# Two-layer attention trunk on one core: a chunk's last two key blocks are transposed and evicted together

## The chip, the cores and the metric

One core of one Trainium2 chip runs the whole program. The metric is the device time of one execution in microseconds (us). The engines are named as in the profile: PE is TensorE, DVE is VectorE, ACT is ScalarE, POOL is GpSimd, SP is the engine that issues the DMAs; SPq and the like are an engine's queue. PEld is the loading of weights into PE.

## What is computed

The input is 1024 positions of 1024 channels; 16 learned positions are put in front, which makes 1040. Two layers follow. Each one normalizes, projects, runs two kinds of attention heads side by side, gates them with SiLU, projects back and adds to the residual. Cut to what matters here:

```python
# differential heads (4 per layer): two softmaxes, one subtracted from the other
s = einsum(q, k) * scale;  s = where(chunk(k) <= chunk(q), s, -inf)
p = softmax(s);            a = p[:, :, 0] - lam * p[:, :, 1]
do = rmsnorm(a @ v, subln_gain) * (1 - lam_init) * silu(dg)
# forgetting heads (8 per layer): causal, with a cumulative bias
s = einsum(q, k) * scale + c[q] - c[k];  s = where(k <= q, s, -inf)
fo = (softmax(s) @ v) * silu(fg)
h = h + concat(do, fo) @ w_out
```

All of it is float32; the kernel splits most operands of a product into a high and a low part (float32r) and adds two or three products.

## The kernel before, in words

**Tiling.** The 1040 positions are nine blocks, 80 and then seven of 128 and a last one of 64 (`BS`, `BE`, lines 29 and 30). Three blocks are a chunk (`CS`, `CE`): 336, 384 and 320 positions. Eight head pairs are worked through in each layer, pairs 0 to 3 differential and 4 to 7 forgetting. A `Unit` (line 664) is one chunk of queries of one differential head pair, or of one head of a forgetting pair: 12 and 24 units a layer, 72 in all.

**A unit.** `scores` (628) makes the scores of one query block against all its keys on PE, DVE adds the mask or bias, takes the running minimum and evicts (652, 656), and ACT takes the exponential with its row sum (660). For a forgetting head DVE takes the reciprocal (692) and POOL scales the rows (693). For a differential head there are two such passes, m = 0 and m = 1; after the second DVE takes a reciprocal (709), makes one factor per row from it, lambda and the first row sum (710), and combines the two (712). Then, for each key block j of the unit (three, six or nine of them), `transp` (727) turns the probabilities of the unit's query blocks on PE into a PSUM tile `tp`, ACT copies this to `ath`, the high part (743), and DVE subtracts to get `atl`, the low part (744). `av` (748) multiplies both with the values and adds into `po`. A chunk's last two key blocks see only part of the queries. Their products are still 256 columns wide, so POOL fills the missing columns with zeros in `ath` and `atl` (741, 742): once in a unit of the first and the second chunk, and twice in one of the third. `finish` (765) evicts `po` into `ta` tiles, of which there are three (`OB`), applies the gate if it is there already (785), and stores to DRAM (786). `head_sums` (793) makes the differential heads' sums of squares on PE and copies three columns out, one by one (803).

**Gates.** `gate` (581) projects a pair's gate. Where the attention of that chunk is already stored, it loads it into a `ta` tile (`load_o`, 591), multiplies on POOL (619) and stores (620). Otherwise it keeps the gate in a `gs` tile; at most `GB`, 4, are kept (602).

**What sets the order.** PE's instructions are in the order in which the program issues them. `attention` (805) walks through the units: the first two transposes, then products and transposes in turn (line 838 and after), with score steps of the next unit put between them; all the steps are offered by `layer` (1080) one at a time. Between them `layer` puts pieces of the other projections (`fills`, 1023, in the order of `ORDER`), as a planner's clock (`Clock`, 160) and costs (lines 52 to 60) say: it fills until the next step's input is due (`need`). The planner charges 0.088 us at each change between transposes and other matmuls (`TURN`) and says that an eviction is ready 0.7 us after its transposes (`LT`). The other engines work in the order in which their own queues were filled.

Of the kernel before, what the change touches and what calls it, by code (L numbers as in the profile page):

```python
# [8 lines left out]
F32 = mybir.dt.float32  # L9
# [24 lines left out]
CE = [336, 720, T]  # L34
CW = 384

WB, XB, QB, EB, AB, GB, OB, TCB = 8, 4, 8, 6, 2, 4, 3, 3
MW = 512
TB, SB = 2, 3

# [44 lines left out]
def trunk_kernel(ctx, tc, x, meta, norm_gain, w_in, fbias, lq1, lk1, lq2, lk2,  # L85
# [18 lines left out]
    for t, r, a in ((dm, 64, MW - 64), (dm0, N_META, N_META)):  # L104
# [12 lines left out]

    qls = [[cp.tile([P, CE[c] - CS[c]], F32R, name=f"ql{c}{s}") for s in range(2)]
           for c in range(3)]
    dma(out=ident, in_=cst[:, C_ID:C_ID + P])  # L120
    for c in range(3):
        for s in range(2):
            nc.gpsimd.memset(qls[c][s][64 - 64 * s:128 - 64 * s, :].bitcast(F32), 0.0)
# [51 lines left out]
    when = {}  # L175

    def mm(o, a, b, start, stop, passes=1):
        n = b.shape[-1]
        nc.tensor.matmul(o, a, b, start=start, stop=stop)  # L179
        pe.add(b.dtype == BF16, max(n * passes * COL, 0.056))  # L180

# [399 lines left out]
    def gate(l, p, acts, box):  # L581


        g0 = (DG if p < 4 else FG) + (p % 4) * P
        ws = load_w_all(w_in[l], [(g0, g0 + P)])
        parts = 1 if p < 4 else 2

        def finished(p, c):
            return sum((p, c, s) in box["fin"] for s in range(parts))

        def load_o(p, c):
            n = finished(p, c)
            if not n:
                return ()
            w = CE[c] - CS[c]
            o = st("ta", CW, F32, OB)
            dma(out=o[0:n * P // parts, :w], in_=oscr[l, c, p, 0:n * P // parts, 0:w])
            return (o,) * n

        for c in range(3):  # L600
            w = CE[c] - CS[c]
            while box["kept"] >= GB:
                yield True
            there = load_o(p, c)
            mb, c0 = [], skip(l, c)
            yield from mtile(ws, acts, c, mb, c0)
            now = finished(p, c)
            if now > len(there):
                there = load_o(p, c)
            pt = mb[0]  # L610
            th = st("tc", CW)
            nc.scalar.activation(th[:, c0:w], pt[:, c0:w], AF.Tanh, scale=0.5)
            keep = len(there) < parts
            g = st("gs", CW, bufs=GB) if keep else th
            nc.vector.scalar_tensor_tensor(g[:, c0:w], th[:, c0:w], 1.0, pt[:, c0:w],
                                           ALU.add, ALU.mult)
            if there:
                o = there[0][0:len(there) * P // parts, c0:w]
                nc.gpsimd.tensor_tensor(o, o, g[0:o.shape[0], c0:w], ALU.mult)
                dma(out=oscr[l, c, p, 0:o.shape[0], c0:w], in_=o)  # L620
                box["done"]["g", c] = pe.t + 2.0
            if keep:
                box["kept"] += 1
                box["gs", p, c] = g
            yield
# [38 lines left out]
    class Unit:  # L664
# [17 lines left out]
        def score(self, j, m):  # L682
            l, ext = self.l, BE[j]
            if j == self.tiles[-1] and (m if self.diff else self.s):
                self.box["sc_ok"].add((self.p, self.c))
            kt = self.box["k", self.p, self.c]
            q = self.box["q", self.p, self.c]
            if not self.diff:
                cb = self.box["cb", self.s]
                e, l, rows = scores(kt, q, self.s, j, ext, lambda a, b: cb[:, a:b], True)  # L690
                r = st("rl", 2, bufs=6)
                nc.vector.reciprocal(r[rows, 0:1], l[rows, :])  # L692
                nc.gpsimd.tensor_scalar(e[rows, :ext], e[rows, :ext], r[rows, 0:1], 1.0,  # L693
                                        ALU.mult, ALU.mult)
                self.at[j] = e, rows
                self.ready = max(self.ready, pe.t + LS[0][0] + LS[0][1] * ext)
                return

            l0 = self.box["l0"][:, self.p, j:j + 1]

            def bias(a, b):
                return dm0[:, a:b] if j == 0 else dm[:, MW - ext + a:MW - ext + b]
            e, ls, rows = scores(kt, q, m, j, ext, bias, False, l0 if m == 0 else None)
            if m == 0:
                self.e0 = e
                return
            e0 = self.e0
            r = st("rl", 2, bufs=6)
            nc.vector.reciprocal(r[rows, 0:1], ls[rows, :])
            nc.vector.scalar_tensor_tensor(r[rows, 1:2], r[rows, 0:1], neglam[rows, l:l + 1],  # L710
                                           l0[rows, :], ALU.mult, ALU.mult)
            nc.vector.scalar_tensor_tensor(e0[rows, :ext], e[rows, :ext], r[rows, 1:2],
                                           e0[rows, :ext], ALU.mult, ALU.add)
            self.at[j] = e0, rows
            self.ready = max(self.ready, pe.t + LS[1][0] + LS[1][1] * ext)

        def geom(self, j):
            c, w = self.c, self.w
            i0 = max(j, 3 * c)
            n0 = BS[i0] - CS[c]  # L720
            n1 = max(min(n0, w - 256), 0) if j > 3 * c else 0
            return BE[j] - BS[j] + self.pad(j), i0, n0, n1

        def pad(self, j):
            return 64 if j == NB - 1 else 0

        def transp(self, j):
            c, w = self.c, self.w
            kz, i0, n0, n1 = self.geom(j)
            tp = att_ps()  # L730
            for i in self.tiles:
                if i < i0:
                    continue
                e, rows = self.at[i]
                o = BS[i] - CS[c] - self.pad(i)
                tr(tp[:kz, o:BE[i] - CS[c]], e[rows, BS[j] - self.pad(j):BE[j]],
                   ident[rows, rows])
            ah = st("ath", CW, F32R, AB)
            al = st("atl", CW, F32R, AB)
            if n1 < n0:  # L740
                nc.gpsimd.memset(ah[:kz, n1:n0].bitcast(F32), 0.0)
                nc.gpsimd.memset(al[:kz, n1:n0].bitcast(F32), 0.0)
            nc.scalar.activation(ah[:kz, n0:w], tp[:kz, n0:w], AF.Copy)  # L743
            nc.vector.tensor_tensor(al[:kz, n0:w], tp[:kz, n0:w], ah[:kz, n0:w].bitcast(F32),  # L744
                                    ALU.subtract)
            self.ev[j] = (ah, al, pe.t + LT)

        def av(self, j):
            w = self.w
            kz, i0, n0, n1 = self.geom(j)  # L750
            if j == 0:
                self.po = ps.tile([P, 512], F32, name="po", tag="po", bufs=1)
            ah, al, _ = self.ev.pop(j)
            v = self.box["v", self.p, j]
            if self.diff:
                vh, vl = v[:kz, j, 0:P], v[:kz, j, P:2 * P]
# [1 line left out]
            else:  # L758
                vs = v[:kz, j, self.s * P:(self.s + 1) * P]
                prods = ((vs, ah), (vs, al))  # L760
            for n, (a, b) in enumerate(prods):
                mm(self.po[:, n1:w], a, b[:kz, n1:w], j == 0 and n == 0,
                   j == self.nblk - 1 and n == len(prods) - 1)

        def finish(self):

# [24 lines left out]
            return late  # L791

    def head_sums(sq, c, p, box):
        ms = box["ms"][:, p, :]
        box["sums"] += 1
        pt = proj_ps("sc")
        for b in range(3):
            j = 3 * c + b
            n = BE[j] - BS[j] + (64 if j == NB - 1 else 0)
            mm(pt[:n, b:b + 1], sq[:, BE[j] - CS[c] - n:BE[j] - CS[c]], ones, True, True, 4)  # L800
        for b in range(3):
            n = BE[3 * c + b] - BS[3 * c + b] + (64 if 3 * c + b == NB - 1 else 0)
            nc.vector.tensor_copy(ms[:n, 3 * c + b:3 * c + b + 1], pt[:n, b:b + 1])

    def attention(l, box):

# [22 lines left out]
        for i, u in enumerate(units):  # L829
# [4 lines left out]
                free = 2 * free - 1  # L834
            if nx and nx.p != u.p and not nx.diff:
                free = 0
            n = u.nblk
            seq = [("t", j) for j in range(TB)]
            for j in range(n):
                seq.append(("a", j))  # L840
                if j + TB < n:
                    seq.append(("t", j + TB))
            nt = 0
            yield u.ready, ("v", u.p, 0)
            box["vp"] = u.p
            for k, (what, j) in enumerate(seq):
# [4 lines left out]
                    u.transp(j)  # L851
                    nt += 1
                else:
                    yield u.ev[j][2], ("v", u.p, j)
                    u.av(j)
                yield 0.0, None
                if todo and (nt == n or (free > 0 and nt >= FR0 and k % FR1 == FR1 - 1)):
# [19 lines left out]
    def head_norms(l, box):  # L877
# [9 lines left out]
        def turn():  # L887
            pt = proj_ps("sc")
            tr(pt[:36, 0:P], rs, ident)
            rt = st("msr", P, bufs=1)  # L890
            nc.scalar.activation(rt[:36, :], pt[:36, 0:P], AF.Copy)
            for h in range(4):
                for j0, j1 in ((0, 1), (1, 8), (8, 9)):
# [219 lines left out]

    with tc.manual_schedule(engines={mybir.EngineType.PE}):
        acts = [None] * 3
        box = {"done": {}, "sc_ok": set(), "fin": set(), "kept": 0, "sums": 0}
        v0 = v_unit(0, 0, acts, box)
        xs = [first_load(0)]
        next(v0)
# [16 lines left out]
        for l in range(depth):  # L1136
# [2 lines left out]
            layer(l, acts, box, new)  # L1139
            tail = box["tail"]  # L1140
            if l < depth - 1:
                acts, box = new, {"done": {}, "sc_ok": set(), "fin": set(), "kept": 0, "sums": 0}
                v0 = weave(v_unit(l + 1, 0, acts, box), tail)
            else:
                drive(tail)
# [54 lines left out]
```

## Time and profile before

| | us |
|---|---|
| runs of the kernel, median of 3 | 1608.13 (1601.7 to 1608.35) |
| the profiled execution: its time | 1607.66 |
| the profiled execution: its span, first to last instruction | 1605.6 |
| busy DVE, ACT, POOL | 1043.0, 828.6, 689.6 |

The span is what the trace covers; some 2 us lie around it. A busy time is the sum of an engine's instructions. Matmuls are pipelined, so that PE's busy time counts overlaps, and its cost is better read from the starts of neighbours. The granted clock of PE has a mean of 0.973 over the span. The stages are: 0 to 90 us the input and the first values, 90 to 400 differential heads and 400 to 700 forgetting heads of the first layer, to 870 its output projection; then the same again, 870 to 1190, 1190 to 1480 and to the end.

### The profile page before, as it was taken

What the parts mean: (1) busy time and instruction counts of PE and PEld (TensorE: products, weight loads), DVE (VectorE), ACT (ScalarE), POOL (GpSimd) and SP (SyncE); (2) the same over time, 40 slices, a digit from 0 to 9 for tenths busy, and PEclk for the clock granted to TensorE, in tenths of its full rate; (3) what the DMA queues carried; (4) which work ended last, traced back from release to release, by engine and by line L of the source; (5) the groups of instructions that cost most, each with busy time, mean ns of one, the idle gap of its engine ahead of it and who ended that gap; (6) DMA issues with size and microseconds to landing.
All of it is one profiled execution on the core that took longest, in us unless ns stands there. A gap on an engine that the chain in (4) does not pass through costs nothing. (4 is left out here: it accounts for less than half of the span.)

```text
span 1605.6 us, 30162 instructions
## 1 busy us (share of the span) xinstructions
PE 1487.7 (93%) x9932; PEld 1420.1 (88%) x9932; DVE 1043.0 (65%) x3024; ACT 828.6 (52%) x2067; POOL 689.6 (43%) x1125
## 2 busy tenths in 40 slices
PE   5988999999999999988998999899999999888997
PEld 4888989999999999887988899799999999886897
DVE  6488747866755575757655976586756555547564
ACT  6455545545654565543334654465556556446443
POOL 3353233404442445456846341442253344344674
PEclk9999999999999999998999999999999999999999
DMA  9252212223321324555434231332242222335454
GB/s 242 64 113 73 71 51 75 72 36 86 69 66 42 79 67 126 170 151 159 147 70 106 69 87 33 88 81 50 43 93 59 52 69 61 87 96 159 138 158 139
DMA packets 181725, 148.28 MB, mean 92 GB/s; under 512 B 19624, under 2 KB 177120, under 8 KB 181568
## 3 DMA queue, kind: packets, MB, share of 16 engines
q1 hardware_dynamic: 181568, 146.34, 34.6%
q8 instruction: 79, 1.29, 0.3%
q14 instruction: 78, 0.64, 0.1%
HBM read 117.70 MB, written 28.59 MB: 91 GB/s over the span
## 5 line engine op out<-in xcount | busy, mean ns | idle before, releaser
L179 PE MATMUL pj<-acth,whi 128*128 128x320 f32 (+2 forms) x1536 | 517.0, 337 | 22.9 <-ACT tc L416 7.6
L179 PE MATMUL pj<-acth,wlo 128*128 128x320 f32 (+2 forms) x1536 | 498.1, 324 | 2.7 <-POOL wlo L263 2.7
L179 PE MATMUL pj<-actl,whi 128*128 128x320 f32 (+2 forms) x1536 | 497.8, 324 | 0.0
L263 POOL TENSOR_TENSOR wlo<-wst,whi 128x256 fp32r<-128x256 f32 (+1 forms) x320 | 249.3, 788 | 244.0 <-ACT whi L259 216.3
L179 PEld LDWEIGHTS pj<-acth,whi 128*128 128x128 f32 x1536 | 295.9, 193 | 28.0 <-ACT tc L416 8.2
L179 PEld LDWEIGHTS pj<-acth,wlo 128*128 128x128 f32 x1536 | 295.2, 192 | 3.8 <-POOL wlo L263 3.2
L179 PEld LDWEIGHTS pj<-actl,whi 128*128 128x128 f32 x1536 | 293.9, 191 | 0.0
L660 ACT ACTIVATE e<-e,mn 80x80 f32<-80x80 f32 (+8 forms) x288 | 225.2, 782 | 124.2 <-DVE mn L652 121.6
L744 DVE TENSOR_TENSOR atl<-tp,ath 128x320 fp32r<-128x320 f32 (+8 forms) x432 | 191.5, 450 | 97.7 <-ACT ath L743 92.9
L743 ACT ACTIVATE ath<-tp 128x320 fp32r<-128x320 f32 (+8 forms) x432 | 167.6, 403 | 138.2 <-PE tp L183 131.1
L179 PE MATMUL sc<-kt,qq 128*128 128x296 f32 (+9 forms) x480 | 178.8, 375 | 25.2 <-DVE mn L652 17.3
L259 ACT ACTIVATE whi<-wst 128x256 fp32r<-128x256 f32 (+1 forms) x304 | 124.1, 415 | 150.4 <-DMA wst<-in_w_out_dram 50.7
L693 POOL TENSOR_SCALAR e<-e,rl 80x80 f32<-80x80 f32 (+2 forms) x144 | 110.8, 770 | 165.6 <-DVE rl L692 160.2
L183 PE MATMUL tp<-ident,e 128*128 128x128 f32 (+2 forms) x1080 | 180.7, 275 | 0.9 <-POOL e L693 0.8
L179 PE MATMUL po<-ath,v 128*128 128x256 f32 (+5 forms) x576 | 167.1, 331 | 13.2 <-ACT ath L743 9.9
L179 PE MATMUL pj<-whi,acth 128*128 128x256 f32 (+3 forms) x576 | 166.4, 289 | 6.7 <-DVE v L428 5.8
L179 PE MATMUL pj<-wlo,acth 128*128 128x256 f32 (+3 forms) x576 | 164.2, 285 | 2.1 <-POOL wlo L263 1.4
L179 PE MATMUL pj<-whi,actl 128*128 128x256 f32 (+3 forms) x576 | 163.8, 284 | 0.6 <-POOL actl L404 0.6
L179 PE MATMUL sc<-kt,ql 128*128 128x296 f32 (+9 forms) x480 | 159.7, 335 | 0.0
L179 PE MATMUL po<-atl,v 128*128 128x256 f32 (+5 forms) x432 | 136.8, 317 | 12.8 <-DVE atl L744 11.7
L183 PEld LDWEIGHTS tp<-ident,e 128*128 128x128 f32 (+2 forms) x1080 | 137.1, 140 | 7.0 <-POOL e L693 2.3
L179 PEld LDWEIGHTS sc<-kt,qq 128*128 128x128 f32 (+1 forms) x480 | 91.5, 191 | 37.7 <-DVE mn L652 23.8
(166 smaller groups left out, 2471.5 us busy)
## 6 DMA issues: line engine op xcount, KB each, us to landing
wst<-in_w_in_dram SPq DMA_DIRECT2D x256, 128.0 KB
wst<-in_w_out_dram SPq DMA_DIRECT2D x192, 128.0 KB
cb<-cscr SPq DMA_DIRECT2D x16, 520.0 KB
cb<-in_rope_dram SPq DMA_DIRECT2D x20, 320.0 KB
cb<-in_rope_dram SPq DMA_DIRECT2D x16, 384.0 KB
oscr<-ta SPq DMA_DIRECT2D x22, 192.0 KB
oscr<-ta SPq DMA_DIRECT2D x26, 160.0 KB
cb<-in_rope_dram SPq DMA_DIRECT2D x12, 336.0 KB
```

Source lines behind the costliest of these rows:

```text
L179: nc.tensor.matmul(o, a, b, start=start, stop=stop)
L183: nc.tensor.transpose(o, a, idn)
L259: nc.scalar.activation(hi, sg_, AF.Copy)
L263: eng.tensor_tensor(lo, sg_, hi.bitcast(F32), ALU.subtract)
L660: nc.scalar.activation(e[rows, :ext], e[rows, :ext], AF.Exp, scale=-1.0, bias=mn[rows, len(pcs) - 1:len(pcs)], accum_out=l[rows, :])
L693: nc.gpsimd.tensor_scalar(e[rows, :ext], e[rows, :ext], r[rows, 0:1], 1.0, ALU.mult, ALU.mult)
L743: nc.scalar.activation(ah[:kz, n0:w], tp[:kz, n0:w], AF.Copy)
L744: nc.vector.tensor_tensor(al[:kz, n0:w], tp[:kz, n0:w], ah[:kz, n0:w].bitcast(F32), ALU.subtract)
```

## The change

Key blocks n-2 and n-1 of a unit become one group: their transposes go into one PSUM tile side by side (block n-1 behind column w), one ACT copy and one DVE subtraction evict both. The two parts lie in fixed tiles `ats`, in which stretches of zeros are written once at the start; a product that needs zero columns reads them from there, for block n-1 as two stretches of 128 columns. POOL's clearing for each unit goes. The product of lambda and the first row sum is made on POOL after pass m = 0, so that DVE has a reciprocal and a product of two columns left. `head_sums` makes all three columns 128 rows high and copies them with one instruction. A gate loads the stored attention once, after its matmuls and not before them, and `GB` goes from 4 to 3 (2 for the last two chunks of pair 7). `turn` takes its tile from the ring `tc`.

```diff
-WB, XB, QB, EB, AB, GB, OB, TCB = 8, 4, 8, 6, 2, 4, 3, 3
+WB, XB, QB, EB, AB, GB, OB, TCB = 8, 4, 8, 6, 2, 3, 3, 3
...
+    ats = [cp.tile([P, 2 * CW + 192], F32R, name=f"at{i}") for i in range(AB)]
+    AH, AL = 128, CW + 192
     dma(out=ident, in_=cst[:, C_ID:C_ID + P])
+    for t in ats:
+        nc.gpsimd.memset(t[:, 0:AH].bitcast(F32), 0.0)
+        nc.gpsimd.memset(t[:, AL - 64:AL].bitcast(F32), 0.0)
...
-            while box["kept"] >= GB:
+            while box["kept"] >= (GB - 1 if p == 7 and c else GB):
                 yield True
-            there = load_o(p, c)
             mb, c0 = [], skip(l, c)
             yield from mtile(ws, acts, c, mb, c0)
-            now = finished(p, c)
-            if now > len(there):
-                there = load_o(p, c)
+            there = load_o(p, c)
...
             if m == 0:
-                self.e0 = e
+                r = st("rl", 2, bufs=6)
+                nc.gpsimd.tensor_scalar(r[rows, 0:1], l0[rows, :], neglam[rows, l:l + 1], 1.0,
+                                        ALU.mult, ALU.mult)
+                self.e0 = e, r
                 return
-            e0 = self.e0
-            r = st("rl", 2, bufs=6)
-            nc.vector.reciprocal(r[rows, 0:1], ls[rows, :])
-            nc.vector.scalar_tensor_tensor(r[rows, 1:2], r[rows, 0:1], neglam[rows, l:l + 1],
-                                           l0[rows, :], ALU.mult, ALU.mult)
+            e0, r = self.e0
+            nc.vector.reciprocal(r[rows, 1:2], ls[rows, :])
+            nc.vector.tensor_tensor(r[rows, 1:2], r[rows, 1:2], r[rows, 0:1], ALU.mult)
...
-        def transp(self, j):
+        def groups(self):
+            n = self.nblk
+            return [(j,) for j in range(n - 2)] + [(n - 2, n - 1)]
+
+        def transp(self, g):
             c, w = self.c, self.w
             tp = att_ps()
+            n0 = BS[max(g[0], 3 * c)] - CS[c]
+            kz = BE[g[0]] - BS[g[0]]
             for i in self.tiles:
                 e, rows = self.at[i]
                 o = BS[i] - CS[c] - self.pad(i)
+                for j in g:
+                    if i >= j:
+                        oo = o if j == g[0] else w
+                        k0 = BS[j] - self.pad(j)
+                        tr(tp[:kz, oo:oo + BE[i] - CS[c] - o], e[rows, k0:k0 + kz],
+                           ident[rows, rows])
-            ah = st("ath", CW, F32R, AB)
-            al = st("atl", CW, F32R, AB)
-            if n1 < n0:
-                nc.gpsimd.memset(ah[:kz, n1:n0].bitcast(F32), 0.0)
-                nc.gpsimd.memset(al[:kz, n1:n0].bitcast(F32), 0.0)
+            n1 = w if len(g) == 1 else w + BE[g[1]] - BS[g[1]] + self.pad(g[1])
+            t = ats[self.box["at"] % AB]
+            self.box["at"] += 1
+            ah, al = (t[:kz, x:x + n1 - n0] for x in (AH, AL))
+            nc.scalar.activation(ah, tp[:kz, n0:n1], AF.Copy)
+            nc.vector.tensor_tensor(al, tp[:kz, n0:n1], ah.bitcast(F32), ALU.subtract)
...
+                self.ev[g[0]] = (n0 - z, *(t[:kz, x - z:x + w - n0] for x in (AH, AL)), ready)
+            if len(g) == 2:
+                two = []
+                for x in (AH, AL):
+                    v = t[:kz, 0:P]
+                    two.append(bass.AP(v.tensor, v.offset,
+                                       [list(v.ap[0]), [x + w - n0, 2], [1, P]]))
+                self.ev[g[1]] = (w - 256, *two, ready)
...
-        for b in range(3):
-            n = BE[3 * c + b] - BS[3 * c + b] + (64 if 3 * c + b == NB - 1 else 0)
-            nc.vector.tensor_copy(ms[:n, 3 * c + b:3 * c + b + 1], pt[:n, b:b + 1])
+            a = BE[j] - P - CS[c] if j == NB - 1 else BS[j] - CS[c]
+            mm(pt[:, b:b + 1], sq[:, a:a + P], ones, True, True, 4)
+        nc.vector.tensor_copy(box["ms"][:, p, 3 * c:3 * c + 3], pt[:, 0:3])
...
-            n = u.nblk
-            seq = [("t", j) for j in range(TB)]
-            for j in range(n):
-                seq.append(("a", j))
-                if j + TB < n:
-                    seq.append(("t", j + TB))
+            gs = u.groups()
+            n = len(gs)
+            seq = [("t", g) for g in gs[:TB]]
+            for i, g in enumerate(gs):
+                seq += [("a", j) for j in g]
+                if i + TB < n:
+                    seq.append(("t", gs[i + TB]))
```

## Rows read from the trace of the kernel before

**Rows 1.** Busy time of each engine and its share of the span, from the page
```profile
PE 1487.7 (93%) x9932; PEld 1420.1 (88%) x9932; DVE 1043.0 (65%) x3024; ACT 828.6 (52%) x2067; POOL 689.6 (43%) x1125
```

**Rows 2.** Windows view, first differential stage: us, then busy us (instructions) by engine
```profile
90.00:400.00 310.00, 290.16 (x1964) 279.53 (x1962) 228.26 (x683) 162.86 (x414) 105.51 (x161) 0.98 0.28 69
```

**Rows 3.** Waits of PE in attention: total us, times, longest
```profile
PE sc L179 <- DVE mn L652: 17.3, 15, 3.8
PE po L179 <- DVE atl L744: 11.7, 14, 2.3
PE po L179 <- ACT ath L743: 9.9, 7, 3.6
PE sc L179 <- DVE e L656: 6.3, 7, 1.3
PE po L179 <- DVE ta L782: 3.1, 2, 2.4
```

**Rows 4.** Groups by form, PE: products of 256 columns (busy, mean ns, idle before)
```profile
L179 PE MATMUL po<-ath,v 128*128 128x256 f32 x192 | 49.3, 298 | 1.0 <-ACT ath L743 1.0
L179 PE MATMUL po<-atl,v 128*128 128x256 f32 x144 | 40.9, 285 | 1.9 <-POOL atl L742 1.0 <-DVE atl L744 0.8
```

**Rows 5.** Timeline of PE around one lone transpose: start, duration, instruction
```profile
410.47 0.27 PE L183 MATMUL tp<-ident,e 128*128 128x128 f32 x1
410.50 0.38 PE L179 MATMUL sc<-kt,qq 128*128 128x296 f32 x1
410.72 0.30 PE L179 MATMUL sc<-kt,ql 128*128 128x296 f32 x1
410.86 0.30 PE L179 MATMUL sc<-kt,qq 128*128 128x296 f32 x1
```

**Rows 6.** Groups by form, ACT and VectorE: evictions of the transposed blocks
```profile
L743 ACT ACTIVATE ath<-tp 128x384 fp32r<-128x384 f32 x72 | 35.0, 486 | 18.7 <-PE tp L183 17.4 <-DVE mn L652 0.7
L743 ACT ACTIVATE ath<-tp 128x256 fp32r<-128x256 f32 x48 | 18.1, 377 | 3.4 <-PE tp L183 3.1
L743 ACT ACTIVATE ath<-tp 128x128 fp32r<-128x128 f32 x48 | 13.0, 272 | 19.1 <-PE tp L183 18.6
L744 DVE TENSOR_TENSOR atl<-tp,ath 128x384 fp32r<-128x384 f32 x72 | 39.7, 551 | 0.4 <-ACT ath L743 0.2
L744 DVE TENSOR_TENSOR atl<-tp,ath 128x256 fp32r<-128x256 f32 x48 | 20.0, 416 | 1.7 <-ACT ath L743 1.5
L744 DVE TENSOR_TENSOR atl<-tp,ath 128x128 fp32r<-128x128 f32 x48 | 13.7, 285 | 3.5 <-ACT ath L743 3.3
```

**Rows 7.** Groups by form, VectorE: steps of one column
```profile
L710 DVE SCALAR_TENSOR_TENSOR rl<-rl,neglam,l 128x1 f32<-128x1 f32 x64 | 19.1, 299 | 1.3
L803 DVE COPY ms<-sc 128x1 f32<-128x1 f32 x64 | 6.4, 148 | 8.1 <-PE sc L179 8.0
```

**Rows 8.** GpSimd: clearing, its waits, the weights' low part, the gate's product
```profile
L741 POOL MEMSET ath<- 128x128 f32 x48 | 9.9, 206 | 97.2 <-PE po L179 91.8 <-DVE kt L428 3.0 <-DVE mn L652 2.0
POOL ath L741 <- PE po L179: 141.1, 48, 23.6
L263 POOL TENSOR_TENSOR wlo<-wst,whi 128x256 fp32r<-128x256 f32 (+1 forms) x320 | 249.3, 788 | 244.0 <-ACT whi L259 216.3 <-issue 16.1 <-PE pj L179 2.9
L619 POOL TENSOR_TENSOR ta<-ta,tc 128x320 f32<-128x320 f32 x18 | 17.0, 946 | 26.2 <-DMA ta<-oscr 8.0 <-DVE ffz L530 7.5 <-issue 6.1
```

**Rows 9.** Waits view: the sum of two heads waiting for a free tile
```profile
DVE ta L782 <- DMA oscr<-ta: 6.2, 3, 3.2
```

**Rows 10.** Timeline among the last gates of layer 1
```profile
1421.05 0.48 DVE L782 TENSOR_TENSOR ta<-po,ta 64x320 f32<-64x320 f32 x1 [1.29 <-DMA oscr<-ta]
...
1422.11 0.44 PE L179 MATMUL pj<-acth,whi 128*128 128x384 f32 x1 [2.50 <-DVE gs L615]
```

**Rows 11.** Timeline, one differential pair: end of the first exponential, reciprocal after the second
```profile
333.98 0.19 ACT L660 ACTIVATION_READ_ACCUMULATOR e<-e,mn 128x1 f32 x1
...
336.26 0.16 DVE L709 RECIPROCAL rl<-ls 128x1 f32<-128x1 f32 x1
```

## What the change should do to the time

> **What bounds the kernel now.** I read the page's first part, then the stages, then what PE waits for, then single groups. PE is busy 93% of the span, and no other engine more than 65% [rows 1]. Even in the differential stage, where DVE has most to do, DVE is busy 228.3 of 310 us and PE 290.2 [rows 2]. So the end is set by PE's own stream, and the change can move it in two ways only: by PE work, or by PE's waits. The waits that the change can reach are small. PE waits 17.3 + 6.3 = 23.6 us for DVE to empty score tiles, 9.9 + 11.7 = 21.6 us for evictions of transposed blocks, and 3.1 us for `ta` [rows 3]. The whole sum is 48.3 us, 3.0% of the span, and it is the ceiling.
>
> **The parts.** The sum is made against the profiled execution, 1607.66 us (span 1605.6, and some 2 us around it); it stands 0.5 us under the median of 1608.13, so I count both as the same start.
>
> *Fewer runs of transposes.* Each of 72 units has one run less, but not one transpose less: block n-1 still needs the same query blocks turned. What is a run worth by itself? At a lone transpose PE goes from its start to the second matmul after it in 410.72 - 410.47 = 0.25 us, and the next step of that shape takes 410.86 - 410.72 = 0.14 us. So a run of one costs 0.11 us, all of it [rows 5]. The planner charges two turns of 0.088 for each run, 72 x 0.176 = 12.7 us in all, and thinks it has saved that. On the chip it could be nothing if a transpose costs 0.11 us in any run, or at most the whole 0.11 per run, 7.9 us. I take 0, because the number of transposes stays.
>
> *One eviction for two.* In the first two chunks ACT's 377 + 272 ns become 486, DVE's 416 + 285 become 551 [rows 6]. ACT sheds 0.163 us, DVE 0.150, in 72 units 11.7 and 10.8 us (the third chunk, with other widths, priced the same). That is engine time beside PE. What PE gets is its waits at these blocks, and they can be separated: every product of the last two blocks is 256 columns wide, every other is wider. Before all 336 of them PE was idle 1.0 + 1.9 = 2.9 us, and 1.0 of that is for POOL's clearing [rows 4]. So nearly all the 21.6 us lie at earlier blocks, which the change leaves as they are. I take 2 of the 2.9.
>
> [...]
>
> The price is that the joint eviction is later for block n-2: ACT and DVE need 0.109 and 0.135 us more [rows 6], and the lone transpose of 0.11 us [rows 5] no longer stands between. Block n-2 thus loses 0.35 us of cover per unit, 25 us in 72 if nothing hid it. The cover is the score steps and other projections between transposes and product, and it is ample so far: 2.9 us of idle in 336 products [rows 4]. I take +1 and keep 0 and +25 as ends, near the low one.
>
> *Clearing on POOL.* 192 memsets (96 pairs) at about 0.206 us go, 39.6 us, and with them 141.1 us in which POOL stood at its head waiting for PE to release the tile [rows 8]. Queued behind were weights' low parts, copies of q, row scalings and gate products. But PE's own waits for `tp`, `po` and `sc` in [rows 3] name DVE and ACT. The 1.0 us at `atl` is counted above; I take 0.5 more, between 0 and 3.
>
> *One-column steps.* On DVE, 72 differential score pairs still have two such steps; only the second is simpler. It took 0.299 us, and at a copy's 0.148 it would shed 72 x 0.15 = 10.9 us; at least 0. The copies of `head_sums` go from 72 to 24, 48 x 0.148 = 7.1 us [rows 7]. POOL gets 72 products of one column, which the trace does not have: between a memset's 0.206 and a `wlo`'s 0.788 [rows 8], 15 to 57 us, and near the memset, being one column. All of DVE's savings, 10.8 + 5 + 7.1, are some 23 us, 2% of its 1043. If PE's 23.6 us of waits for score tiles fell by a tenth, that is 2 us; the bounds are 0 and 8 (a third). I take 2.
>
> *The gate's load later, once.* A load of stored attention now takes its `ta` tile after the gate's matmuls. Before, it held one of three from before them, while `finish` wanted two. DVE waited 6.2 us in three places for a store from `ta` [rows 9]. One of these ends at 1421.05; the gate's product on DVE stood behind it, and PE stopped for 2.50 us [rows 10]. With PE's 3.1 us for `ta` [rows 3] that is 5.6 us; I take 3, between 0 and 5.6. On SP the loads move behind some weight loads; on POOL the gate's product can wait for its load, and a `wlo` behind it. The nearest row is an 8.0 us wait of a gate product for its load [rows 8]. It is no row of PE's, so I charge nothing, with +3 as the end.
>
> *`GB` 3, `tc` for `turn`, fixed tiles, wider sums.* A gate of pair 7 may be held back, and another takes its place in the fill. If none is left PE waits; the nearest row is a stop of 2.50 us at these gates [rows 10]. 0, up to +3. The matmuls of `head_sums` still have one moving column, 0.
>
> Sum: 0 - 2 + 1 - 0.5 - 2 - 3 = -6.5 us, so 1607.66 - 6.5 = 1601.2, rounded to **1601.5 us**. About 0.5% (8 us) is what a measurement of this kernel can tell from no change, so the likeliest outcome is just inside it.
>
> **Rivals.**
> 1. *Nothing arrives.* The order on PE is made anew, since the planner counts fewer turns, and PE meets its waits in other places. For: the reachable waits [rows 3] are single stops of up to 3.8 us that hang on what happens to be queued. Against: every engine has less to do. 1608, give or take 4.
> 2. *Wide relief.* With the memsets' 141.1 us of blocking gone and DVE 23 us lighter, half of the 23.6 us for score tiles and a third of the 21.6 for evictions go too: 11.8 + 7.2, and `ta` in full, 5.6, less the 3 of late loads. 1607.66 - 21.6 = 1586. For: DVE is busy three quarters of the differential stage [rows 2]. Against: many stops come from single ACT or DVE queues behind a DMA [rows 9].
> 3. *Slower: POOL between two passes.* DVE's last one-column step now waits for POOL's product. In the pair shown the first exponential ends at 334.17 and the reciprocal after the second starts at 336.26, so POOL has about 2.1 us [rows 11]. If its queue is longer than that, DVE stops, with the evictions of the next scores behind it. It decides where two or three `wlo` of 0.788 us stand ahead, or one that itself waits for ACT (216.3 us of such waits) [rows 8]. At one `wlo` late per pair DVE loses 72 x 0.788 = 57 us; if a quarter reaches PE, +14 on the 1601.5: 1616. Against: that margin, and fewer memsets in the queue.
>
> [...]
>
> 4. *Slower: cover or reading form.* Block n-2 waits in earnest (up to 25 us, above), or the two-stretch operand is read more slowly: 168 products, each at worst as two matmuls of 0.11 us for 0.12, so +0.1 each, 17 us. 1618.
>
> That the change does not do what it says holds in one point: the differential steps on DVE do not get fewer.
>
> **Chances and range.** The forecast 0.44, nothing arrives 0.22, wide relief 0.20, POOL between 0.10, cover or form 0.04. Under 1600 lie wide relief and somewhat under two fifths of the forecast: 0.20 + 0.17 = 0.37 faster. Over 1616 lie the two slow cases and a corner of the second: 0.15. Within 0.5% remain 0.48. The likeliest case by itself gives 1595 to 1608; with wide relief at 1586 and the POOL case at 1616 the range is 1586 to 1616.
>
> **What would show it.** Right: 360 evictions of `at`, those of 384 columns near 486 and 551 ns; no memsets in the units; PE's work unchanged; idle before 256-column products still some 3 us; no DVE wait for a store from `ta`. Wrong: DVE or ACT idle for POOL's `rl`, PE idle growing at the 256-column products of block n-2, or a fall of PE's score waits by more than 8 us.

## The result, and the profile after

The changed kernel takes **1618.56 us** (median of 6 runs, 1615.9 to 1622.6) against 1604.81 for the kernel before, timed beside it: a ratio of 1.0085, 95% interval 1.0063 to 1.0107. It is slower by 13.8 us, where 1601.5 was predicted and the range ended at 1616. The profiled execution took 1615.9 us, the lowest of the six, with a span of 1614.1 and a mean granted clock of 0.970 (before 0.973). The one before stands 2.9 us above its median. So the two traces differ by 8.5 us of span (1614.1 - 1605.6), and the rest of the 13.8 us is in neither.

The page of the changed kernel, busy time of each engine, answers to [rows 1]:

```profile
PE 1495.9 (93%) x9932; PEld 1423.6 (88%) x9932; DVE 1026.9 (64%) x2904; ACT 816.7 (51%) x1995; POOL 681.8 (42%) x1009
```

PE issues 9932 matmuls in both kernels, but is busy 8.2 us more with them (1495.9 against 1487.7). DVE is busy 16.1 us less, ACT 11.9, POOL 7.8. So all three helping engines have less to do, and still the end is later. The single parts arrived. Groups by form and waits of the changed kernel, for [rows 4, 6 to 9]:

```profile
L749 ACT ACTIVATE at<-tp 128x384 fp32r<-128x384 f32 x120 | 57.8, 482 | 31.7 <-PE tp L189 26.5 <-DVE tc L427 2.9 <-DVE at L750 1.6
L750 DVE TENSOR_TENSOR at<-tp,at 128x384 fp32r<-128x384 f32 x120 | 66.0, 550 | 4.6 <-ACT at L749 4.2
L185 PE MATMUL po<-at,v 128*128 128x256 f32 x336 | 66.3, 303 | 6.9 <-ACT at L749 4.8 <-DVE at L750 2.0
L709 POOL TENSOR_SCALAR rl<-l,neglam 128x1 f32<-128x1 f32 x64 | 25.9, 405 | 161.3 <-ACT e L663 154.3 <-DMA wst<-in_w_in_dram 2.9 <-DMA oscr<-ta 2.5
L715 DVE TENSOR_TENSOR rl<-rl 128x1 f32<-128x1 f32 x64 | 12.8, 199 | 5.2 <-POOL rl L709 0.8 <-DVE rl L714 0.5
L820 DVE COPY ms<-sc 128x3 f32<-128x3 f32 x24 | 3.7, 154 | 1.3 <-PE sc L185 1.2
DVE rl L715 <- POOL rl L709: 1.7, 2, 0.9
POOL ta L622 <- DMA ta<-oscr: 19.3, 5, 5.1
```

The evictions cost what [rows 6] said. The one-column product takes POOL 405 ns and DVE's second step 199 instead of 299. POOL now stands 154.3 us at the head of its queue for the exponential's sum, where it stood 141.1 us for PE [rows 8]; DVE waits for POOL's product only twice, 1.7 us. No wait of DVE for a store from `ta` is left [rows 9]. The idle time before the products of 256 columns went from 2.9 to 6.9 us.

What PE waits for, by name, in the changed kernel, for [rows 3]:

```profile
PE po L185 <- DVE at L750: 15.7, 19, 1.9
PE po L185 <- ACT at L749: 15.3, 8, 3.5
PE pj L185 <- DVE hc L948: 12.2, 5, 5.6
PE sc L185 <- DVE mn L655: 11.8, 8, 3.8
PE sc L185 <- DVE e L659: 4.3, 7, 1.3
```

The waits for score tiles fell from 23.6 to 16.1, those for evictions rose from 21.6 to 31.0. Together PE's idle time is the same as before: 1614.1 - 1495.9 = 118.2 us against 1605.6 - 1487.7 = 117.9. So in this pair of traces the totals show no added standing: PE takes 8.2 us longer over as many matmuls (overlapping ones count once in its busy time: 192 of 298 ns on average make 49.3 us in [rows 4]). Part of it is the granted clock. In both traces it stands at 1.00 or at 0.50 and nowhere between, at 0.50 for 98.2 us against 87.1 before, of which PE is busy 77.0 and 72.7. A projection matmul of 384 columns is followed there by the next start after 0.320 us, at 1.00 after 0.175 (medians). So the 4.3 us more of PE's work are worth, by an estimate from these numbers, 2 of the 8.2; the other 6 were not split further.

The stages show where. The windows view, PE only, cut where the first product of heads 4 to 6 and of pair 7 and the last product of attention start (columns: us, PE busy, granted clock, DMA share, GB/s); the kernel before, from layer 0's heads 4 to 6 to the end of layer 1's output projection, without layer 1's differential heads:

```profile
403.00:632.00 229.00, 228.81 (x1602) 1.00 0.28 73
632.00:713.00 81.00, 71.23 (x442) 0.92 0.52 148
713.00:887.00 174.00, 154.54 (x946) 0.93 0.46 125
...
1180.00:1424.00 244.00, 234.32 (x1622) 0.99 0.28 71
1424.00:1505.00 81.00, 72.98 (x450) 0.92 0.43 125
1505.00:1596.00 91.00, 85.46 (x553) 0.98 0.52 156
```

and the changed kernel, the same stages:

```profile
406.00:638.00 232.00, 227.58 (x1585) 1.00 0.29 71
638.00:716.00 78.00, 68.69 (x420) 0.91 0.48 141
716.00:895.00 179.00, 160.32 (x983) 0.93 0.48 126
...
1188.00:1421.00 233.00, 228.22 (x1587) 0.99 0.27 71
1421.00:1504.00 83.00, 71.12 (x434) 0.90 0.42 122
1504.00:1605.00 101.00, 92.39 (x593) 0.97 0.50 148
```

Two things stand out. Before, layer 1's heads 4 to 6 take 244 us, and layer 0's, with 20 matmuls less, 229. The changed kernel takes 233 there, 11 us less, with 35 matmuls fewer (1587 for 1622). But its pair 7 and output projection of layer 1 take 83 + 101 = 184 us against 81 + 91 = 172, 12 us more: fewer matmuls in pair 7 (434 for 450), more of them after it (593 for 553), which is projection work that the fill left over. What was won in one stage is given back in the next, in part as the same work done later. In layer 0, heads 4 to 6 add 3 us, the stages behind them 2 and what lies ahead of them 3. That makes some 9 us, the 8.5 of the spans.

PE's waits inside these stages. The kernel before, layer 1, heads 4 to 6 (first four lines), then pair 7:

```profile
PE pj L179 <- DVE gs L615: 2.9, 2, 2.5
PE po L179 <- DVE ta L782: 2.4, 1, 2.4
PE pj L179 <- DVE tc L615: 2.2, 2, 1.2
PE pj L179 <- DVE ql L430: 1.6, 1, 1.6
...
PE po L179 <- DVE atl L744: 3.2, 4, 2.3
PE po L179 <- ACT ath L743: 1.4, 2, 1.0
```

The changed kernel, layer 1, pair 7 (two lines) and the output projection (one):

```profile
PE po L185 <- ACT at L749: 5.7, 2, 3.5
PE po L185 <- DVE at L750: 5.0, 5, 1.9
...
PE pj L185 <- DVE hc L948: 6.9, 2, 5.6
```

Before, a cluster of stops at the last projections and gates ahead of pair 7 holds PE up. After, PE stands at pair 7's evictions, with less fill to put between, and later at the output projection: by the windows it is idle 12 and 9 us in these two stages, against 8 and 6 before.

### The profile page after: what moved, and what is told of

Same layout as the page of the kernel before. It is cut to its first block, busy times and chain, and to the rows that moved or that the text cites. A ratio compares the mean times of both kernels' runs of the same rounds, so it can differ in the third digit from the quotient of the medians.

```text
span 1614.1 us, 29760 instructions
## 1 busy us (share of the span) xinstructions
PE 1495.9 (93%) x9932; PEld 1423.6 (88%) x9932; DVE 1026.9 (64%) x2904; ACT 816.7 (51%) x1995; POOL 681.8 (42%) x1009
## 5 line engine op out<-in xcount | busy, mean ns | idle before, releaser
L185 PE MATMUL po<-at,v 128*128 128x320 f32 (+5 forms) x1008 | 235.9, 329 | 31.9 <-DVE at L750 15.7
L750 DVE TENSOR_TENSOR at<-tp,at 128x384 fp32r<-128x384 f32 (+2 forms) x360 | 182.8, 513 | 79.7 <-ACT at L749 75.8
L749 ACT ACTIVATE at<-tp 128x384 fp32r<-128x384 f32 (+2 forms) x360 | 155.8, 453 | 116.3 <-PE tp L189 108.7
L185 PEld LDWEIGHTS po<-at,v 128*128 128x128 f32 (+1 forms) x1008 | 166.0, 196 | 42.7 <-DVE at L750 23.8
L189 PE MATMUL tp<-ident,e 128*128 128x128 f32 (+2 forms) x1080 | 169.6, 277 | 0.0
L269 DVE TENSOR_TENSOR wlo<-wst,whi 128x256 fp32r<-128x256 f32 (+1 forms) x128 | 82.5, 649 | 66.9 <-POOL whi L267 50.8
```

Of the source, the lines that this page charges most:

```text
L189: nc.tensor.transpose(o, a, idn)
L269: eng.tensor_tensor(lo, sg_, hi.bitcast(F32), ALU.subtract)
L749: nc.scalar.activation(ah, tp[:kz, n0:n1], AF.Copy)
L750: nc.vector.tensor_tensor(al, tp[:kz, n0:n1], ah.bitcast(F32), ALU.subtract)
```

## The experiments

All were timed in five rounds beside the kernel before, whose median then was 1605.6 to 1607.4 us. A ratio is against it. Windows and waits come from one profiled execution of each kernel, which can lie some us off its median.

**Is it the planner's clock?** *e1_charge* gives the planner back the two turns of each unit that the change took off its clock. Nothing that any engine computes is different; only the order is, PE's and with it that of the other queues.

```diff
 nc.vector.tensor_tensor(al, tp[:kz, n0:n1], ah.bitcast(F32), ALU.subtract)
+if len(g) == 2:
+    pe.t += 2 * TURN
 ready = pe.t + LT
```

> The changed kernel, with the planner charged two turns (0.176 us) at each joint transposes group, as it was charged for the last block's own run before; nothing else differs. Theory A, the planner's clock: it saw 12.7 us less attention and so left 36 projection matmuls a layer to be done after the attention, where they stand in a stretch with longer waits; then this run comes back to 1603 to 1609. Theory B, gates (three kept, load after the matmuls): stays at 1616 to 1620. Theory C, POOL's product between the two passes: stays at 1616 to 1620. Theory D, the joint eviction arrives late at the product: stays too. The matmuls after the attention should fall back from 924 and 492 to about 888 and 456 only if A's step is as described.

1601.09 us, 0.997 (0.9957 to 0.9984). In its windows the output stages hold 951 and 560 matmuls where the changed kernel has 983 and 593: less is left behind, as Theory A said. *e4_uncharged* does the opposite alone, on the kernel before; the eviction is told due so much earlier, too.

```diff
+if j == self.nblk - 1:
+    pe.t -= 2 * TURN
 self.ev[j] = (ah, al, pe.t + LT)
```

> The kernel before, with two turns (0.176 us) taken off the planner's clock at each unit's last block, which is the change's step in the planner alone; every operation is as before. Theory A: slower than before, 1611 to 1619, with some 30 matmuls a layer moved behind the attention. Theories B, C and D: 1602 to 1608, no difference.

1633.71 us, 1.0171 (1.0147 to 1.0195). So 12.7 us of bookkeeping, no instruction added or removed, cost the old form 28 us and the new one 17.5. Three more kernels ask what in the clock does it. *e6_pace* leaves the charge off and shortens the attention that the planner is told; *e9_ready_only* makes only the joint eviction due two turns later; *e8_double* charges four turns.

```diff
-ATT = [26.3] * 4 + [36.0] * 4
+ATT = [25.8] * 4 + [34.9] * 4      # e6_pace
...
-ready = pe.t + LT
+ready = pe.t + LT + 2 * TURN * (len(g) == 2)      # e9_ready_only
...
+if len(g) == 2:
+    pe.t += 4 * TURN      # e8_double
```

> The changed kernel, with the planner's stated length of a head pair's attention (ATT) cut by what the change took off its clock: 26.3 to 25.8 us for three units, 36.0 to 34.9 for six; the clock itself stays uncharged. Theory A1, pace: the fill is spread over an attention that is shorter than ATT says, so it falls behind and is left over; then this run comes back to 1600 to 1608, with some 888 and 456 matmuls after the attention. Theory A2, order: what counts is where the clock stands when the next products and scores are asked for, not how much fill is spread; then it stays at 1613 to 1620.

1601.54 us, 0.9958 (0.9943 to 0.9973).

> The changed kernel, with the joint eviction said to be ready 0.176 us later in the plan, and no charge on the planner's clock itself. Theory D (the joint eviction arrives late) and A2: most of the 17 us between the changed kernel and the charged one come back, 1600 to 1608. Theory A1: no, since the fill's pace is as in the change: 1613 to 1620.

1602.01 us, 0.9967 (0.9955 to 0.9979).

> The changed kernel with four turns (0.352 us) charged for each joint group and not two. If the charge of two turns happens to hit a good order (any other order would be worse by chance), this is 1605 to 1620. If the time goes with the charge, because more of the fill is done inside the attention, it is 1595 to 1601.

1599.57 us, 0.9952 (0.9938 to 0.9965). Each of them brings the new form to 1600 to 1602. That the order is the cause is shown. That it is a matter of pace (how fast the planner gives out the fill) is not: e9 leaves as much projection work behind as the changed kernel (its pair 7 and output of layer 1 take 82 + 101 us) and takes 1602 us all the same, by 10 us less in heads 4 to 6 of the two layers. Its windows, heads 4 to 6 of layer 0, then the last three of layer 1:

```profile
405.00:632.00 227.00, 226.36 (x1580) 1.00 0.29 70
...
1182.00:1410.00 228.00, 226.85 (x1594) 1.00 0.27 72
1410.00:1492.00 82.00, 69.47 (x423) 0.88 0.43 129
1492.00:1593.00 101.00, 93.10 (x598) 0.95 0.51 149
```

**The parts alone.** *e5_gates* is the kernel before with only the gate part (`GB` 3, one load after the matmuls). In the traces PE's 9932 matmuls stand in the order of before, one by one, so this run changes a part and not PE's order.

```diff
-WB, XB, QB, EB, AB, GB, OB, TCB = 8, 4, 8, 6, 2, 4, 3, 3
+WB, XB, QB, EB, AB, GB, OB, TCB = 8, 4, 8, 6, 2, 3, 3, 3
-            while box["kept"] >= GB:
+            while box["kept"] >= (GB - 1 if p == 7 and c else GB):
-            there = load_o(p, c)
...
-            now = finished(p, c)
-            if now > len(there):
-                there = load_o(p, c)
+            there = load_o(p, c)
```

> The kernel before, with the change's three steps for gates alone: three kept and not four, two for the last chunks of pair 7, the load once and after the matmuls. Theory B: 1612 to 1619. Theories A, C and D: 1600 to 1608; the forecast's own step for the ta tiles would give 1602, 3 us less.

1601.04 us, 0.9969 (0.9955 to 0.9983): 4.6 us faster. Its windows and waits:

```profile
1181.00:1419.00 238.00, 232.21 (x1623) 1.00 0.29 73
...
DVE ta L779 <- DMA oscr<-ta: 1.5, 1, 1.5
```

The wait for a store falls from 6.2 us [rows 9] to 1.5, and the stage with the cluster from 244 to 238: PE's stop of 2.4 us at `ta` is gone there, those at `tc`, `ql` and `gs` stay, 5.3 us in all. *e3_rl_on_dve* is the changed kernel with lambda's product back on DVE; *e7_charge_dve* is e1 with the same edit. In the traces PE's matmuls stand in the order of the changed kernel in e3, in that of e1 in e7.

```diff
-                nc.gpsimd.tensor_scalar(r[rows, 0:1], l0[rows, :], neglam[rows, l:l + 1], 1.0,
-                                        ALU.mult, ALU.mult)
...
+            nc.vector.scalar_tensor_tensor(r[rows, 1:2], r[rows, 0:1], neglam[rows, l:l + 1],
+                                           l0[rows, :], ALU.mult, ALU.mult)
```

> The changed kernel, with the product of lambda and the row sum back on DVE as before, so nothing of a score pair runs on POOL. Theory C (POOL in front of DVE): 1604 to 1609, and the 154 us in which POOL stands waiting for an exponential are gone. Theories A, B, D: 1615 to 1620, since PE's order is the same instruction for instruction; at most 2 us of difference.

1614.53 us, 1.0048 (1.003 to 1.0066), 4 us less than the changed kernel, with intervals that just meet.

> The changed kernel with the planner charged as before, and lambda's product back on DVE. If the two effects add, 1601.1 less 4 us (1618.6 to 1614.5 was the product's move alone): 1597. If POOL's product cost something only in the plan that is not charged: 1601.

1600.8 us, 0.9949 (0.9934 to 0.9965), against 1601.09 and 0.997 for e1. POOL's product is not the cause; by the medians it may cost 4 us in one order and next to nothing in another, by the ratios 6 and 3.

**Is the order of the changed kernel an unlucky one?** Two steps that could not mend a clock running ahead: a longer told attention, and another slack.

```diff
-ATT = [26.3] * 4 + [36.0] * 4
+ATT = [26.8] * 4 + [37.1] * 4      # e10_slow_pace
...
-CMAX, SLACK, RMIN, RMAX, STEP, FR0, FR1 = 3.17, 0.4, 0.03, 2.52, 2, 2, 2
+CMAX, SLACK, RMIN, RMAX, STEP, FR0, FR1 = 3.17, 0.45, 0.03, 2.52, 2, 2, 2      # e11_slack; 0.5 in e16_slack50
```

> The changed kernel with the planner told a longer attention (26.8 and 37.1 us for each chunk in place of 26.2 and 36.0), so that it paces the fill slower. If the loss is a matter of pace (too little fill given out in attention because the clock of the plan runs ahead), this makes it worse: 1618 to 1626 us. If the plan of the changed kernel is one unlucky order and almost any other order is free of it, 1600 to 1606 us.

1605.43 us, 0.9993 (0.9973 to 1.0012); the 26.2 of the expectation is 26.3 in the code.

> The changed kernel with the planner's slack at 0.45 us in place of 0.4, a step that is neutral as to pace and only makes some choices fall out differently. Pace: as the changed kernel, 1614 to 1619 us. One unlucky order: 1600 to 1606 us.

1596.99 us, 0.994 (0.9917 to 0.9963).

> The changed kernel with the planner's slack at 0.5 us. If the changed kernel is at 1597 to 1606 us in nearly every order but its own, 1597 to 1606 us. If slow orders are common in it, or if the uncharged clock makes it slow as a rule and 0.45 was the lucky one, 1612 to 1622 us.

1603.03 us, 0.9987 (0.9973 to 1.0002). A longer told attention helps (e10), a shorter one too (e6), and so does another slack (e11, e16); so pace falls. *e12_uncharged_pace* is e4 with the shorter told attention of e6.

> The kernel before with two turns fewer charged on the planner's clock for each chunk's last block (which alone gave 1633.7 us), and the told attention shortened by as much as the clock lost (25.8 and 34.9 us). Pace: the plan's clock and its told length agree again, 1603 to 1610 us. If it is the order of the particular plan: anything, with no return expected, about 1615 to 1635 us.

1597.79 us, 0.9945 (0.9925 to 0.9965), 36 us under e4 and under both ranges that were written. Then the same steps on the kernel before, with nothing of the change: slack 0.45 (*e14*), 0.35 (*e15*), and the told attention of e6 (*e17*).

> The kernel before with the planner's slack at 0.45 us in place of 0.4: none of the change, another order. If only the order of the changed kernel is an outlier and the plan of before is an ordinary one, 1600 to 1610 us. If any new order moves the time by ten us either way, it may lie anywhere from 1597 to 1634 us, with over 1612 or under 1598 as the sign of it.

1591.31 us, 0.9915 (0.9902 to 0.9928).

> The kernel before with the planner's slack at 0.35 us. As for 0.45: an ordinary plan, 1600 to 1610 us; a wide draw, over 1612 or under 1598 us.

1620.25 us, 1.0101 (1.0088 to 1.0114).

> The kernel before with the told attention at 25.8 and 34.9 us for each chunk (the same step that took the changed kernel from 1618.6 to 1601.5 us). If that step only mends a clock that runs ahead, it has nothing to mend here and does harm or nothing: 1603 to 1615 us. If it makes any plan better by pacing the fill closer, 1590 to 1600 us.

1614.63 us, 1.0069 (1.0053 to 1.0085). The wide draw (any new order can move the time by ten us or more) was right: 0.05 us of slack moves the old form by 14 us down or 15 up, as much as the whole change did. And e6's step, which brought the changed kernel 17 us, costs the kernel before 9.

**Where in the program?** e14, layer 1, heads 4 to 6, and e15, layer 0 and layer 1:

```profile
1176.00:1406.00 230.00, 229.59 (x1613) 1.00 0.29 74
```

```profile
399.00:640.00 241.00, 232.60 (x1605) 0.99 0.27 70
...
1193.00:1437.00 244.00, 234.25 (x1617) 0.99 0.28 70
```

In the old form the time goes with the number of layers in which the cluster of stops stands (heads 4 to 6 of layer 0 and 1, us, in the order of their times; e17's stages are of an execution of 1608.1 us):

| kernel | layer 0 | layer 1 | time |
|---|---|---|---|
| e14 | 230 | 230 | 1591.3 |
| e18 (below) | 229 | 230 | 1592.7 |
| e12 | 230 | 231 | 1597.8 |
| e5 | 230 | 238 | 1601.0 |
| before | 229 | 244 | 1605 to 1607 |
| e17 | 246 | 246 | 1614.6 |
| e15 | 241 | 244 | 1620.3 |
| e4 | 243 | 241 | 1633.7 |

*e18_before_layer1* tests it: the kernel before with the other slack in layer 1 alone.

```diff
-            while credit > 0 or pe.t < need - SLACK:
+            while credit > 0 or pe.t < need - SLACK - 0.05 * l:
```

> The kernel before with the slack at 0.45 us in layer 1 alone; layer 0's order is that of before. If the cluster of PE stops at the end of layer 1's heads 4 to 6 (9.7 us idle in the kernel before, 0.4 with 0.45 in both layers) is what lies between 1605 and 1591 us, and 0.45 takes it away here too, 1590 to 1595 us, with that stage near 230 us in place of 243. If the gain of 0.45 was spread over both layers, 1597 to 1603 us.

1592.68 us, 0.9909 (0.9897 to 0.9922). The windows of layer 1, heads 4 to 6, pair 7 and output:

```profile
1179.00:1409.00 230.00, 229.55 (x1613) 1.00 0.30 74
1409.00:1488.00 79.00, 71.53 (x445) 0.94 0.46 137
1488.00:1582.00 94.00, 89.19 (x567) 0.96 0.52 153
```

PE's matmuls stand in the order of before up to 1196 us, 16 us into this stage. The stage falls from 244 to 230 us, with 9 matmuls less, which come later; the rest of layer 1 stays at 173 against 172, and the whole gains 13 us. This is shown to be one place. For the new form, *e13_pair7* raises the fill that the planner allots to pair 7 in both layers, *e19_pair7_layer1* in layer 1 alone.

```diff
-FADD = [0.0, 0.0, 0.0, 0.0, 0.0, 0.0, 0.0, 20.0]
+FADD = [0.0, 0.0, 0.0, 0.0, 0.0, 0.0, 0.0, 26.4]      # e13_pair7; in e19 the 6.4 are added where l is 1
```

> The changed kernel with the fill paced closer in the last head pair alone (its allowance 26.4 us in place of 20.0). If the loss lies in the last pair, where fill is thin and PE's granted clock falls, 1602 to 1608 us. If it is spread over all pairs, 1614 to 1620 us.

1605.29 us, 1.0003 (0.9986 to 1.0019).

> The changed kernel with the closer pace of the last head pair in layer 1 alone; layer 0's order is that of the changed kernel. The run with it in both layers took 7.7 us off layer 1's last pair and output stage and 1.6 us off layer 0's. If the loss sits there, 1606 to 1611 us here. If the 13 us of that run were a scatter over the whole program, 1613 to 1619 us.

1607.53 us, 1.0003 (0.9986 to 1.0019). In e19, layer 1's pair 7 and output:

```profile
1424.00:1506.00 82.00, 72.83 (x475) 0.98 0.46 136
1506.00:1596.00 90.00, 85.52 (x555) 0.96 0.53 157
```

172 us against the changed kernel's 184, and a granted clock of 0.98 in pair 7 against 0.90. PE's order is that of the changed kernel up to 1441 us, 20 us into pair 7. So 11 us by the medians (1618.6 - 1607.5) can be had at this one place; between the changed kernel and e1 lie 17.5. It is not the only one: e9 and e16 leave 183 and 185 us there and take 1602.0 and 1603.0, by 455 and 450 us in heads 4 to 6 of both layers against the changed kernel's 465.

**The best version** is e14, the kernel before with one constant altered: 1591.3 us (four executions), faster than both kernels. Whether the gate part on top of it gains more was not tried.

## Why the prediction was wrong

**The step that failed** is the first term of the sum, "the planner charges two turns of 0.088 for each run, 72 x 0.176 = 12.7 us in all, and thinks it has saved that", of which "I take 0, because the number of transposes stays". That is right for the work and wrong for the time: the planner orders PE by that clock, and 12.7 us off it are another order. Its price was 17.5 us here (1618.6 against 1601.1 in e1) and 28 us on the old form (e4). Rival 1 named the mechanism, "The order on PE is made anew, since the planner counts fewer turns", and gave it 1608 "give or take 4"; the size was off, and the sum had no term for it. The runs show 1591 to 1634 for orders of the old form and 1597 to 1619 for the new one, where nine of ten lie under 1608 and the changed kernel's own alone above. The reachable waits of 48.3 us [rows 3] were no ceiling either: the new orders moved PE's waits and the granted clock too. In the two profiled executions PE's idle time stayed and its busy time grew by 8.2 us; between e1 and the changed kernel both grew, idle from 110.0 to 118.2 us and busy from 1485.0 to 1495.9, at mean clocks of 0.976 and 0.970.

Point by point:

- *Transposes*: 0 was right for the work. From the start of a run of one, two, three or six transposes to the second matmul behind it the kernel before takes 0.264, 0.379, 0.484 and 0.850 us (medians of the trace's starts at the full granted clock), the changed one 0.482 and 0.847 for three and six. That is 0.11 to 0.12 us for each transpose and nothing to see for a run.
- *Joint eviction*, -2 + 1: idle before the products of 256 columns went from 2.9 to 6.9 us in the changed kernel, but to 3.5, 0.8, 5.7, 5.8 and 8.8 in e1, e6, e9, e8 and e13; in orders of the old form it lies between 0.5 (e14) and 4.1 (e17), and in e5, with PE's order of before, it is 5.1. So neither the lost cover nor the gain can be told from the order. On ACT the engine time was as worked out, 11.9 us less against 11.7; on DVE the evictions shed 8.7 (191.5 to 182.8), not 10.8.
- *Clearing on POOL*, -0.5: the 141.1 us of standing went, and 154.3 us for the exponential came in its place. No row of PE shows either.
- *One-column steps*, -2: DVE is 16.1 us lighter, not 23. Its second step, at 199 ns and not 148, sheds 6.6 us in all (21.7 to 15.1), the copies 3.3 and not 7.1 (7.0 to 3.7), the evictions the 8.7 above; other groups take some 2.5 more. PE's waits for score tiles are 7.5 us fewer in the changed kernel, and this does not hang on the order alone: in the changed kernel, e1, e6, e8, e9, e11 and e13 they come to 14.9 to 19.1 us, in the kernel before, e4, e14, e15 and e17 to 18.8 to 25.4. Which part brings it, and what it is worth in time, was not separated.
- *Gate*, -3: shown in the order of before. e5 has it at -4.6 us with the 6.2 us wait cut to 1.5. POOL waits 19.3 us for loads in the changed kernel against 8.0 [rows 8], but 2.0 in e5, beside PE.
- *Rival 3* (POOL between two passes): DVE waits for POOL 1.7 us in the changed kernel, in two places, and 7.6 us in e1, in four; e3 and e7 put the price at 0 to 6 us, not 14. One product takes POOL 405 ns where DVE's step of one column takes 199; the two are not the same operation.
- *Rival 4* (the reading form): not so. At the full granted clock a product with the two-stretch operand is followed by the next start after 0.118 us in the changed kernel (median of 160), and so is one with a single stretch, as before. That the measured 1618.6 meets this rival's 1618 is chance.
- *Rival 2* (wide relief): not seen; the lowest order of the new form is 1597.0, 11 us above it.

So the sum for the parts, -6.5 us, can be neither confirmed nor refuted beyond the gate's share: both forms scatter by 10 us or more with the order, and 1605 for the kernel before is a draw as well. That e1 comes to 1601.1, beside the forecast's 1601.5, is luck too. With equal constants the new form is once slower by 14 us (as changed), once by 6 (e11 against e14), and once faster by 13 (e6 against e17). What stays open is which rule of the planner makes a good order. e4 loses 13 us more than e15 by the medians with the same two stages; of the 10 us between their traces, 9 lie in layer 1's pair 7 and output, 83 + 97 us against 78 + 93.

## What to carry to other kernels

Where a planner with a clock sets the order, an edit of its costs is an edit of the program: count what it takes off the clock, and give the forecast the spread that small, neutral steps of the planner's constants cause. Time a few such orders of both kernels before the change is judged by one of each. Then cut the profile by stage: a gain of 11 us and a loss of 12 lay side by side here, and no total of waits showed them.

## What was not expected

- A stage loses more than its stops: the cluster in layer 1's heads 4 to 6 shows 9.1 us of stops in four lines, and in e18 the stage is 14 us shorter. Some 9 of these are idle time; the rest is busy time, of 9 matmuls that moved out and of a stretch at the lower of the clock's two levels: the granted clock is 0.50 from 1399.0 to 1402.4 us, after 9 us of which PE was busy 5.5. How the rest splits was not worked out.
- POOL's one-column product takes 405 ns, twice the 206 of a whole 128x128 memset [rows 8].
- Executions of one kernel may spread by the order too: four of e14 lay between 1589.4 and 1591.5 us, twelve of e19 between 1600.8 and 1613.7. So few do not settle it.
